# Program order for ScalarE, VectorE and GpSimd in the seven-product groups of a decoder trunk, with bank reads ahead of operand preparation

## The chip, the cores and the metric

The kernel runs on one core of one Trainium2 chip. The metric is device time of one execution in microseconds (us). The engines are TensorE (PE in the profile; PEld are its weight loads), VectorE (DVE), ScalarE (ACT), GpSimd (POOL) and SyncE (SP), which issues most loads. Each engine takes its instructions from a queue of its own, in the order in which the built program has them, and waits on semaphores for the others.

## The reference, cut to what matters

Two layers work on a stream of 512 tokens by 1024 features. The part that the change touches is the gated feed-forward block:

```python
gu = x @ w_gate_up[l]                                  # 1024 -> 2 x 2816
hidden = jax.nn.silu(gu[..., :D_FF]) * gu[..., D_FF:]
x = _layer_norm(DEEPNORM_ALPHA * x + hidden @ w_down[l], ln2_g[l], ln2_b[l])
```

All is float32. To keep that precision on TensorE the kernel splits every operand in a high and a low part and makes three matmuls of each product: high x high, high x low and low x high.

## The kernel before

The program runs each layer as a list of weight units of 128 x 1024 floats. For each unit SyncE loads a raw tile (`wraw`, L177 or L179), ScalarE casts it to its high part (`whi`, L204), and VectorE subtracts to get the low part (`wlo`, L137, the helper `lo_of` that all low parts share). There are five raw tiles and five pairs of high and low parts, and preparation runs four operands ahead of TensorE: `used()` is called after each product and prepares the next operand in line.

Of the 22 feature tiles of 128 in the gate and in the up projection, the first two are computed plainly. The other twenty are done two at a time, in ten groups of a layer, each with **seven products** where eight would be usual. A group takes a 2 x 2 arrangement of weight blocks: the two halves of the 1024 inputs, by gate and up. The raw tiles are f (first half, gate), e (second half, up), m (first half, up) and g (second half, gate). The operands come from them in place (L189 to L195):

| product, in TensorE's order | operand | made by | bank |
|---|---|---|---|
| p1 | B11 = f | load | a |
| p3 | B22 = e | load | e |
| p5 | T1: f += m | VectorE L189 | c |
| p7 | T3: m += e | VectorE L191 | d |
| p6 | T2: f += e | VectorE L193 | b |
| p2 | B21 = g | load | a, added on |
| p4 | T4: f += g | GpSimd L195 | d, added on |

f is one tile through T1, T2 and T4, so each sum must wait until the cast and the low part of the one before it have read f. Each product is 24 matmuls (L305). The function `quad_ev` reads the banks (name of the product, then line): p1 L928 and p5 L930, copies by ScalarE to `qa`; p7 L932, VectorE, which takes bank d from the copy of c; p6 L935, VectorE, then L936 and L938 on GpSimd, with the read of bank e (L937, VectorE) between them; p2 L940, silu by ScalarE; p4 L943, VectorE, L944, silu by ScalarE, and two multiplies on GpSimd into the hidden tiles (L950). For the last three hidden tiles of a layer the multiply is L953, and ScalarE (L955) and VectorE (L137, `hd_late`) split the result at once. p4 adds onto bank d, so it can't start before L932 has read it.

What sets the order: TensorE and SyncE run in the order in which the code is written (`manual_schedule`). ScalarE, VectorE and GpSimd are ordered by a scheduler when the program is built, within what the data allow. GpSimd and VectorE share the work on the raw tiles: L195 writes f, so it waits for the low part of T2.

Of the kernel before, what the change touches and what calls it, by code (L numbers as in the profile page):

```python
# [13 lines left out]
ALU = mybir.AluOpType  # L14
# [11 lines left out]
FT = DFF // P  # L26
# [82 lines left out]
def decoder_trunk(ctx: ExitStack, tc: tile.TileContext, wall, xT_in, x_in, pvec, lnp, rtab, out):  # L109
    nc = tc.nc  # L110
# [11 lines left out]
    def main_bank():  # L122
        return psm.tile([P, 512], F32, tag="m", name="pm")

    def aux_bank():
        return psa.tile([P, 512], F32, tag="a", name="pa")

    def scratch(shape, name):
        return reg.tile(shape, F32, tag="sc", name=name, bufs=4)

    def bigpair(which, name):
        h = big.tile([P, KT, S], F32R, tag=f"{which}h", name=f"{name}h")
        l = big.tile([P, KT, S], F32R, tag=f"{which}l", name=f"{name}l")
        return h, l

    def lo_of(out_lo, full, hi):
        nc.vector.tensor_tensor(out=out_lo, in0=full, in1=hi.bitcast(F32), op=ALU.subtract)  # L137
# [60 lines left out]
    def prep_to(n):  # L198
        while state["prep"] < min(n, total, state["used"] + NRING):
            i = state["prep"]  # L200
            kind, unit = operands[i]
            r = operand_of(kind, unit)
            hi = wp.tile([P, UNIT], F32R, tag="hi", name="whi")
            nc.scalar.copy(hi, r)  # L204
            lo = None
            if kind == "I":
                half = lambda t: t.rearrange("p (k m) -> p k m", k=KT)[:, :, P // 2 :]
                lo_of(half(hi), half(r), half(hi))
            else:
                lo = wp.tile([P, UNIT], F32R, tag="lo", name="wlo")  # L210
                lo_of(lo, r, hi)
            prep_t[i] = (hi, lo)
            for k in ends.get(i, ()):
                del raw_t[k]
            state["prep"] += 1
            issue_dma(state["dma"] + NRAW - len(raw_t))

    def take():
        i = state["next"]
        state["next"] += 1  # L220
        prep_to(i + 1)
        return prep_t.pop(i)

    def used(n=1):
        state["used"] += n
        prep_to(state["used"] + LOOK)
# [4 lines left out]
    def slot():  # L231
        while side:
            try:
                next(side[0])
                return
            except StopIteration:
                side.popleft()
# [47 lines left out]
    def quad(xh, xl, sh, sl, ev):  # L285


        t1, t2 = slice(0, S // 2), slice(S // 2, S)
        banks = {n: main_bank() if n != "b" else aux_bank() for n in "aecdb"}
        x1, x2 = slice(0, 4), slice(4, 8)  # L290
        for name, act, bank, first in (("p1", (x1, t1), "a", True), ("p3", 3, "e", True), ("p5", 0, "c", True),
                                       ("p7", 2, "d", True), ("p6", 1, "b", True), ("p2", (x2, t1), "a", False),
                                       ("p4", (x2, t2), "d", False)):
            w = take()
            hi, lo = (t.rearrange("p (j k m) -> p j k m", j=2, k=4) for t in w)
            if isinstance(act, int):
                ah, al = sh[:, act], sl[:, act]
            else:
                ah, al = xh[:, act[0], act[1]], xl[:, act[0], act[1]]
            for j in range(2):  # L300
                pm = banks[bank][:, j * 256 : (j + 1) * 256]
                for k in range(4):
                    go = first and j == 0 and k == 0
                    for n, (x, y) in enumerate(((hi, ah), (hi, al), (lo, ah))):
                        nc.tensor.matmul(pm, lhsT=x[:, j, k], rhs=y[:, k], start=go and n == 0,  # L305
                                         stop=j == 1 and k == 3 and n == 2, skip_group_check=not first)
                slot()
            used()
            ev(name, banks)

    def first_units(evacs):

# [79 lines left out]
    for n in (1, 1, 2, 2, 2):  # L392
        t = scratch([P, n, S], "xraw")
# [136 lines left out]
    for l in range(L):  # L530
# [258 lines left out]
        for b in range(NB):  # L789
            t = scratch([P, DM], "xr")  # L790
# [75 lines left out]
        x1h, x1l = bigpair(oth, f"x1{l}")  # L866
# [11 lines left out]
        def hidden(j):  # L878
            tag = ("vh", "vl", "gt", "oo", "qk")[j // 4]
            if tag not in hf_t:  # L880
                hf_t[tag] = reg.tile([P, 4, S], F32, tag=tag, name=f"hf_{tag}")
            return hf_t[tag], j % 4
# [16 lines left out]
        sh, sl = (t.rearrange("p (s m) (c t) -> p s (m c) t", s=4, c=2) for t in bigpair(cur, f"s{l}"))  # L899
# [22 lines left out]
        def quad_ev(j):  # L922
            t = {}

            def ev(name, banks):
                two = lambda n: t.setdefault(n, scratch([P, 2, S], n))
                if name == "p1":
                    nc.scalar.copy(two("qa")[:, 0], banks["a"])  # L928
                elif name == "p5":
                    nc.scalar.copy(two("qa")[:, 1], banks["c"])  # L930
                elif name == "p7":
                    nc.vector.tensor_tensor(out=two("qb")[:, 1], in0=t["qa"][:, 1], in1=banks["d"], op=ALU.subtract)  # L932
                elif name == "p6":
                    u, v = t["qa"][:, 0], t["qa"][:, 1]
                    nc.vector.tensor_tensor(out=u, in0=banks["b"], in1=u, op=ALU.add)  # L935
                    nc.gpsimd.tensor_tensor(out=v, in0=v, in1=u, op=ALU.subtract)  # L936
                    nc.vector.tensor_tensor(out=t["qb"][:, 0], in0=banks["e"], in1=v, op=ALU.add)  # L937
                    nc.gpsimd.tensor_tensor(out=t["qb"][:, 1], in0=t["qb"][:, 1], in1=u, op=ALU.subtract)  # L938
                elif name == "p2":
                    nc.scalar.activation(two("qc")[:, 0], banks["a"], AF.Silu)  # L940
                elif name == "p4":
                    g = t["qc"]
                    nc.vector.tensor_tensor(out=g[:, 1], in0=banks["d"], in1=t["qa"][:, 0], op=ALU.add)  # L943
                    nc.scalar.activation(g[:, 1], g[:, 1], AF.Silu)  # L944
                    up, g = (x.rearrange("p h (j t) -> p j h t", j=2) for x in (t["qb"], g))
                    for i in range(2):
                        if j + i < NHF:
                            w, n = hidden(j + i)
                            w = w[:, n].rearrange("p (h t) -> p h t", h=2)
                            nc.gpsimd.tensor_tensor(out=w, in0=up[:, i], in1=g[:, i], op=ALU.mult)  # L950
                        else:
                            n = 2 * (j + i - NHF)
                            nc.gpsimd.tensor_tensor(out=up[:, i], in0=up[:, i], in1=g[:, i], op=ALU.mult)  # L953
                            hh, hl = (late[:, n + q].rearrange("p (h t) -> p h t", h=2) for q in range(2))
                            nc.scalar.copy(hh, up[:, i])  # L955
                            lo_of(hl, up[:, i], hh)
            return ev

        for j in range(2, FT, 2):
            quad(x1h, x1l, sh, sl, quad_ev(j))  # L960

        hid = {j: (late[:, 2 * (j - NHF)], late[:, 2 * (j - NHF) + 1]) for j in range(NHF, FT)}
        place = {"next": 0}
# [25 lines left out]
        for b in range(NB):  # L989
            t = scratch([P, DM], "xr2")  # L990
# [103 lines left out]
```

## Time and profile before

| what | value |
|---|---|
| time, median of 3 runs | 1809.02 us (1807.4 to 1809.77) |
| the profiled execution's own time; its span | 1809.39 us; 1807.7 us |
| granted TensorE clock in the span | 0.997 |
| low parts, L137 `wlo` | 380 instructions, mean 1223 ns, 461.3 us busy |
| casts, L204 | 367 instructions, mean 1049 ns, 382.4 us busy |
| matmuls of the groups | L305, 20 groups, in two stretches of the span, from 573.3 and from 1469.2 us |
| GpSimd sums L195 | 20, mean 2535 ns |
| GpSimd L936 and L938 | 20 each, mean 2142 and 1288 ns |

The profile is of one execution on the one core. Its times are from the span's start. A row of the timeline gives start, duration, engine, line, operation, output and inputs, and in brackets the idle time ahead of it with what ended it; "x2" joins two instructions that follow each other. Line numbers are those of the kernel before; behind L938 the changed kernel's differ by one or so, since lines moved.

### The profile page before, as it was taken

Reading aid. Unit: us, or ns where it says so; the run is one execution under the profiler, and the core shown is the slowest. Engines: PE = TensorE matmul, PEld = TensorE weight load, DVE = VectorE, ACT = ScalarE, POOL = GpSimd, SP = SyncE. Lnnn points to the kernel's source line nnn. Section 1 sums busy time; section 2 is a strip of 40 time slices with the busy share of each in tenths; the row PEclk is TensorE's granted clock in tenths of the full one; section 3 lists DMA queues with packets and bytes.
Section 4 is the critical chain, followed back from the end, with each engine's and each line's share of the span. In section 5 each row is a group of like instructions: output and inputs, shape, how many; then the busy total and the mean of one; then the engine's idle time right before and its main releaser. Section 6 shows DMA issues by size and latency. Waiting matters only on the chain.

```text
span 1807.7 us, 24819 instructions
## 1 busy us (share of the span) xinstructions
PE 1783.2 (99%) x10040; PEld 1561.5 (86%) x10040; DVE 1072.7 (59%) x1582; ACT 738.5 (41%) x1056; POOL 298.5 (17%) x245
## 2 busy tenths in 40 slices
PE   9999999999999999999999999999999999999998
PEld 7888888888889999988898888888888899999886
DVE  6655236654459777773476642467535687767634
ACT  4434326554225444451244343356433254444410
POOL 2020000010001444430020100010100014444200
PEclk9999999999999999999999999999999999999999
DMA  7222243234323322363242222422443223322621
GB/s 246 94 82 73 91 153 103 82 129 152 97 93 108 100 94 94 96 220 97 90 163 90 86 82 93 163 82 80 132 162 93 94 94 102 109 94 94 222 70 47
DMA packets 65268, 200.95 MB, mean 111 GB/s; under 512 B 6233, under 2 KB 8153, under 8 KB 63105
## 3 DMA queue, kind: packets, MB, share of 16 engines
q1 hardware_dynamic: 58768, 168.32, 28.6%
q0 software_dynamic: 6384, 31.04, 4.9%
q8 instruction: 79, 1.29, 0.3%
q14 instruction: 37, 0.29, 0.1%
HBM read 186.73 MB, written 12.60 MB: 110 GB/s over the span
## 4 chain that ended last, share of the span: by engine, by line
PE 85%; DVE 6%; POOL 4%; issue 3%; ACT 1%; DMA 0%; SPq 0%; DVEq 0%; POOLq 0%
PE pm L247 10%; PE pm L248 10%; PE pm L249 10%; PE pm L305 10%; PE pm L332 9%; PE pm L334 9%; PE pm L333 9%; PE pa L333 3%; PE pa L332 3%; PE pa L334 3%; DVE wlo L137 2%; PE pa L305 2%; POOL wraw L195 1%; POOL qa L936 1%; PE pa L465 1%
## 5 line engine op out<-in xcount | busy, mean ns | idle before, releaser
L137 DVE TENSOR_TENSOR wlo<-wraw,whi 128x1024 fp32r<-128x1024 f32 (+2 forms) x380 | 461.3, 1223 | 412.5 <-ACT whi L204 410.5
L204 ACT CAST whi<-wraw 128x1024 fp32r<-128x1024 f32 x367 | 382.4, 1049 | 699.2 <-PE pm L248 224.8
L421 POOL TENSOR_TENSOR rs<-ve,nhalf 128x4 f32<-128x4 f32 (+1 forms) x32 | 32.1, 1003 | 639.0 <-DVE ve L420 639.0
L247 PE MATMUL pm<-x20h,whi 128*128 128x512 f32 (+1 forms) x288 | 107.0, 372 | 0.0
L249 PE MATMUL pm<-x20h,wlo 128*128 128x512 f32 (+1 forms) x288 | 105.5, 366 | 0.0
L248 PE MATMUL pm<-x20l,whi 128*128 128x512 f32 (+1 forms) x288 | 105.4, 366 | 0.0
L332 PE MATMUL pm<-whi,x0h 128*128 128x512 f32 x256 | 102.4, 400 | 1.8 <-DVE rvl L137 1.7
L332 PE MATMUL pm<-whi,x20h 128*128 128x512 f32 x256 | 102.4, 400 | 0.6 <-DVE rvl L137 0.6
L334 PE MATMUL pm<-wlo,x20h 128*128 128x512 f32 x256 | 100.4, 392 | 0.0
L334 PE MATMUL pm<-wlo,x0h 128*128 128x512 f32 x256 | 100.3, 392 | 0.0
L333 PE MATMUL pm<-whi,x0l 128*128 128x512 f32 x256 | 100.1, 391 | 0.0
L333 PE MATMUL pm<-whi,x20l 128*128 128x512 f32 x256 | 100.1, 391 | 0.0
L247 PE MATMUL pm<-x0h,whi 128*128 128x512 f32 x232 | 91.9, 396 | 0.0
L249 PE MATMUL pm<-x0h,wlo 128*128 128x512 f32 x232 | 90.5, 390 | 0.0
L248 PE MATMUL pm<-x0l,whi 128*128 128x512 f32 x232 | 90.4, 390 | 0.0
L305 PE MATMUL pm<-x10h,whi 128*128 128x256 f32 x240 | 68.6, 286 | 5.0 <-DVE qb L932 5.0
L305 PE MATMUL pm<-x11h,whi 128*128 128x256 f32 x240 | 68.6, 286 | 5.0 <-DVE qb L932 5.0
L936 POOL TENSOR_TENSOR qa<-qa 128x512 f32<-128x512 f32 x20 | 42.8, 2142 | 163.1 <-DVE qa L935 129.7
L305 PE MATMUL pm<-s1h,whi 128*128 128x256 f32 x240 | 68.4, 285 | 0.0
L305 PE MATMUL pm<-s0h,whi 128*128 128x256 f32 x240 | 68.4, 285 | 0.0
L305 PE MATMUL pm<-s1l,whi 128*128 128x256 f32 x240 | 68.0, 283 | 0.0
L305 PE MATMUL pm<-s1h,wlo 128*128 128x256 f32 x240 | 68.0, 283 | 0.0
(452 smaller groups left out, 4940.7 us busy)
## 6 DMA issues: line engine op xcount, KB each, us to landing
wraw<-wall SPq DMA_DIRECT2D x307, 512.0 KB, 3.6
yd<-sga POOLq DMA_DIRECT2D x4, 1024.0 KB, 5.0
ya<-yd POOLq DMA_DIRECT2D x4, 1024.0 KB, 6.1
gb<-lnp POOLq DMA_DIRECT2D x4, 1024.0 KB, 5.2
x1d<-xr POOLq DMA_DIRECT2D x8, 512.0 KB, 3.0
xr<-x1d POOLq DMA_DIRECT2D x8, 512.0 KB, 4.7
negm<-md POOLq DMA_DIRECT2D x2, 1026.0 KB, 7.2
xr<-xtok POOLq DMA_DIRECT2D x4, 512.0 KB, 4.1
```

The costliest lines, as they stand in the source:

```text
L137: nc.vector.tensor_tensor(out=out_lo, in0=full, in1=hi.bitcast(F32), op=ALU.subtract)
L195: nc.gpsimd.tensor_tensor(out=f, in0=f, in1=g, op=ALU.add)
L204: nc.scalar.copy(hi, r)
L247: nc.tensor.matmul(pm[:, c0:c1], lhsT=hi[:, k], rhs=xh[:, k, c0:c1], start=(k == 0), stop=False)
L248: nc.tensor.matmul(pm[:, c0:c1], lhsT=hi[:, k], rhs=xl[:, k, c0:c1], start=False, stop=False)
L249: nc.tensor.matmul(pm[:, c0:c1], lhsT=lo[:, k], rhs=xh[:, k, c0:c1], start=False, stop=(k == KT - 1))
L305: nc.tensor.matmul(pm, lhsT=x[:, j, k], rhs=y[:, k], start=go and n == 0, stop=j == 1 and k == 3 and n == 2, skip_group_check=not first)
L332: nc.tensor.matmul(pm, lhsT=sh(k)[:, a], rhs=hi[:, j], start=first, stop=False)
L333: nc.tensor.matmul(pm, lhsT=sl(k)[:, a], rhs=hi[:, j], start=False, stop=False)
L334: nc.tensor.matmul(pm, lhsT=sh(k)[:, a], rhs=lo[:, j], start=False, stop=last)
L421: nc.gpsimd.tensor_tensor(out=rs[:, :n], in0=ve[:, :n], in1=nhalf[:, :n], op=ALU.pow)
L936: nc.gpsimd.tensor_tensor(out=v, in0=v, in1=u, op=ALU.subtract)
```

## The change

```diff
@@ quad
                 slot()
+            ev(name, banks)
             used()
-            ev(name, banks)
@@ quad_ev
                     u, v = t["qa"][:, 0], t["qa"][:, 1]
                     nc.vector.tensor_tensor(out=u, in0=banks["b"], in1=u, op=ALU.add)
                     nc.gpsimd.tensor_tensor(out=v, in0=v, in1=u, op=ALU.subtract)
-                    nc.vector.tensor_tensor(out=t["qb"][:, 0], in0=banks["e"], in1=v, op=ALU.add)
                     nc.gpsimd.tensor_tensor(out=t["qb"][:, 1], in0=t["qb"][:, 1], in1=u, op=ALU.subtract)
                 elif name == "p2":
                     nc.scalar.activation(two("qc")[:, 0], banks["a"], AF.Silu)
+                    nc.vector.tensor_tensor(out=t["qb"][:, 0], in0=banks["e"], in1=t["qa"][:, 1], op=ALU.add)
@@ the loop over the groups
-        for j in range(2, FT, 2):
-            quad(x1h, x1l, sh, sl, quad_ev(j))
+        with tc.manual_schedule(engines={mybir.EngineType.Activation, mybir.EngineType.DVE, mybir.EngineType.Pool}):
+            for j in range(2, FT, 2):
+                quad(x1h, x1l, sh, sl, quad_ev(j))
```

In the code a product's banks are now read before the next operand is prepared, and the read of bank e stands with p2 instead of p6. Inside the loop the three scheduled engines now issue in the order of the code. GpSimd's order comes out as it was: L195, two subtractions, two multiplies.

VectorE, before, from the third group into the fourth (`wraw_4933` is the next group's f, `wraw_5100` its m, `wraw_5059` its e; `wlo` rows name the operand's raw tile):

```order
L189 TENSOR_TENSOR wraw_4933<-wraw_4933,wraw_5100 128x1024
L932 TENSOR_TENSOR qb_5195<-qa_5102,pm_5069 128x512
L137 TENSOR_TENSOR wlo_5223<-wraw_5059,whi_5221 128x1024
L191 TENSOR_TENSOR wraw_5100<-wraw_5100,wraw_5059 128x1024
L935 TENSOR_TENSOR qa_5102<-pa_5070,qa_5102 128x512
L137 TENSOR_TENSOR wlo_5256<-wraw_4933,whi_5254 128x1024
L937 TENSOR_TENSOR qb_5195<-pm_5067,qa_5102 128x512
L193 TENSOR_TENSOR wraw_4933<-wraw_4933,wraw_5059 128x1024
L137 TENSOR_TENSOR wlo_5287<-wraw_5100,whi_5285 128x1024
L943 TENSOR_TENSOR qc_5258<-pm_5069,qa_5102 128x512
L137 TENSOR_TENSOR wlo_5327<-wraw_4933,whi_5325 128x1024
```

Three more low parts (B21, T4 and the next B11) stand behind these rows, and then the ring of rows begins again. VectorE now, at the same place (f is `wraw_4937`, m `wraw_5104`, e `wraw_5066`; the read of bank e has line 940 now):

```order
L137 TENSOR_TENSOR wlo_5165<-wraw_4708,whi_5163 128x1024
L932 TENSOR_TENSOR qb_5193<-qa_5097,pm_5071 128x512
L137 TENSOR_TENSOR wlo_5197<-wraw_4937,whi_5195 128x1024
L935 TENSOR_TENSOR qa_5097<-pa_5072,qa_5097 128x512
L137 TENSOR_TENSOR wlo_5228<-wraw_5066,whi_5226 128x1024
L940 TENSOR_TENSOR qb_5193<-pm_5069,qa_5097 128x512
L189 TENSOR_TENSOR wraw_4937<-wraw_4937,wraw_5104 128x1024
L137 TENSOR_TENSOR wlo_5260<-wraw_4937,whi_5258 128x1024
L943 TENSOR_TENSOR qc_5254<-pm_5071,qa_5097 128x512
L191 TENSOR_TENSOR wraw_5104<-wraw_5104,wraw_5066 128x1024
L137 TENSOR_TENSOR wlo_5293<-wraw_5104,whi_5291 128x1024
L193 TENSOR_TENSOR wraw_4937<-wraw_4937,wraw_5066 128x1024
```

The low parts of T2, B21 and T4 follow. L932 now stands directly behind T4's low part, ahead of B11's low part and of L189. L189 moved from ahead of L932 to behind the read of bank e, L191 from ahead of L935 to behind L943, and L193 from ahead of T3's low part to behind it.

ScalarE, before, one round from the cast of the next group's B11:

```order
L204 CAST whi_5420<-wraw_5163 128x1024
L930 COPY qa_5331<-pm_5297 128x512
L204 CAST whi_5450<-wraw_5289 128x1024
L204 CAST whi_5483<-wraw_5163 128x1024
L204 CAST whi_5514<-wraw_5329 128x1024
L940 ACTIVATE qc_5487<-pm_5295 128x512
L204 CAST whi_5555<-wraw_5163 128x1024
L944 ACTIVATE qc_5487<-qc_5487 128x512
L204 CAST whi_5588<-wraw_5362 128x1024
L928 COPY qa_5561<-pm_5525 128x512
```

ScalarE now (the silu of p2 has line 939 now):

```order
L930 COPY qa_5326<-pm_5299 128x512
L204 CAST whi_5392<-wraw_4937 128x1024
L204 CAST whi_5424<-wraw_5167 128x1024
L204 CAST whi_5455<-wraw_5295 128x1024
L939 ACTIVATE qc_5483<-pm_5297 128x512
L204 CAST whi_5487<-wraw_5167 128x1024
L944 ACTIVATE qc_5483<-qc_5483 128x512
L204 CAST whi_5521<-wraw_5333 128x1024
L928 COPY qa_5556<-pm_5527 128x512
L204 CAST whi_5559<-wraw_5167 128x1024
```

The copy of p5 stands ahead of the casts of T4 and B11 instead of behind them; the cast of T1 moved behind the silu of p2, that of T3 behind L944, and that of T2 behind the copy of p1.

VectorE in the ninth group of a layer, now, where the first late hidden tile is made:

```order
L943 TENSOR_TENSOR qc_6631<-pm_6448,qa_6474 128x512
L137 TENSOR_TENSOR hd_late_4606<-qb_6570,hd_late_4606 128x512
L191 TENSOR_TENSOR wraw_6481<-wraw_6481,wraw_6443 128x1024
L137 TENSOR_TENSOR wlo_6672<-wraw_6481,whi_6670 128x1024
L193 TENSOR_TENSOR wraw_6314<-wraw_6314,wraw_6443 128x1024
```

Before, L191 and L193 stood ahead of this L943, and the low part of the late tile came behind that of T2.

## Prediction

> **What bounds the kernel now.** I read the page's head first, then TensorE's waits, then the stage that they point to.
>
> ```profile
> span 1807.7 us, 24819 instructions
> PE 1783.2 (99%) x10040; PEld 1561.5 (86%) x10040; DVE 1072.7 (59%) x1582; ACT 738.5 (41%) x1056; POOL 298.5 (17%) x245
> ```
> ```profile
> PE pm L305 <- DVE qb L932: 10.0, 12, 0.8
> ```
> ```profile
> 573.30:782.50 209.20, 204.21 (x1683) 202.23 (x1682) 153.16 (x142) 95.13 (x118) 88.80 (x47) 1.00 0.31 104
> 1469.20:1678.40 209.20, 204.21 (x1682) 202.16 (x1681) 153.14 (x142) 95.12 (x118) 88.80 (x47) 1.00 0.32 105
> 651.95:673.40 21.45, 20.59 (x168) 20.26 (x168) 15.10 (x16) 9.14 (x12) 9.46 (x5) 1.00 0.28 98
> ```
>
> TensorE is busy nearly throughout. Its one repeated wait in the groups is p4, which must wait until VectorE has read bank d (L932). The windows (length, then PE, PEld, DVE, ACT, POOL) show the ten groups of both layers: 209.20 us each, 20.9 per group, and 21.45 in a later group. The timeline of TensorE says what a group would need:
>
> ```profile
> 587.60 0.28 PE L305 MATMUL pa<-s0h,wlo 128*128 128x256 f32 x1
> ...
> 672.21 0.28 PE L305 MATMUL pm<-x10l,whi 128*128 128x256 f32 x1
> 672.33 0.28 PE L305 MATMUL pm<-x10h,wlo 128*128 128x256 f32 x1
> 673.45 0.39 PE L305 MATMUL pm<-x10h,whi 128*128 128x256 f32 x1 [0.84 <-DVE qb L932]
> ...
> 782.50 0.39 PE L332 MATMUL pa<-whi,hd_pp 128*128 128x512 f32 x1
> ```
>
> A group is 168 matmuls (the third window's count), and without a wait they start 0.12 us apart (672.21, 672.33): 168 x 0.12 = 20.16 us a group, 2.88 for each of its seven products. So the groups lose 209.2 - 201.6 = 7.6 us a layer, 15.2 in all. That is all there is to gain.
>
> Who sets 21.45? The chain of waits over two groups (start, duration) returns to L932 without once passing through TensorE:
>
> ```profile
> 672.72 0.68 DVE qb L932
> ...
> 676.41 2.15 POOL qa L936
> ...
> 679.19 1.68 DVE wraw L193
> ...
> 682.01 0.61 DVE qc L943
> ...
> 684.87 2.27 POOL hf_gt L950
> 687.14 2.37 POOL wraw L195
> ...
> 689.53 1.06 ACT whi L204
> ...
> 694.15 0.68 DVE qb L932
> ```
>
> 694.15 - 672.72 = 21.43. It is a ring of VectorE, GpSimd and ScalarE; TensorE only follows. **The question is what the ring's length becomes, not how soon one bank is read.** The rows of its members:
>
> ```profile
> 601.41 3.42 DVE L137 TENSOR_TENSOR wlo<-wraw,whi 128x1024 fp32r<-128x1024 f32 x1
> ...
> 657.76 1.68 DVE L193 TENSOR_TENSOR wraw<-wraw 128x1024 f32<-128x1024 f32 x1
> 659.37 1.21 DVE L137 TENSOR_TENSOR wlo<-wraw,whi 128x1024 fp32r<-128x1024 f32 x1
> 660.50 0.68 DVE L943 TENSOR_TENSOR qc<-pm,qa 128x512 f32<-128x512 f32 x1
> ...
> 669.18 2.36 DVE L137 TENSOR_TENSOR wlo<-wraw,whi 128x1024 fp32r<-128x1024 f32 x2 [4.63 <-ACT whi L204]
> 671.57 1.22 DVE L189 TENSOR_TENSOR wraw<-wraw 128x1024 f32<-128x1024 f32 x1
> ...
> 675.59 0.68 DVE L935 TENSOR_TENSOR qa<-pa,qa 128x512 f32<-128x512 f32 x1
> 676.19 1.22 DVE L137 TENSOR_TENSOR wlo<-wraw,whi 128x1024 fp32r<-128x1024 f32 x1
> ```
> ```profile
> 579.53 3.30 POOL L195 TENSOR_TENSOR wraw<-wraw 128x1024 f32<-128x1024 f32 x1 [20.84 <-DVE wlo L137]
> ...
> 600.88 2.87 POOL L195 TENSOR_TENSOR wraw<-wraw 128x1024 f32<-128x1024 f32 x1
> ...
> 661.99 3.71 POOL L950 TENSOR_TENSOR hf_gt<-qb,qc 128x512 f32<-128x512 f32 x2 [3.63 <-ACT qc L944]
> 665.67 2.40 POOL L195 TENSOR_TENSOR wraw<-wraw 128x1024 f32<-128x1024 f32 x1
> 676.41 2.14 POOL L936 TENSOR_TENSOR qa<-qa 128x512 f32<-128x512 f32 x1 [8.35 <-DVE qa L935]
> 678.51 1.29 POOL L938 TENSOR_TENSOR qb<-qb,qa 128x512 f32<-128x512 f32 x1
> ```
> ```profile
> 659.55 1.05 ACT L204 CAST whi<-wraw 128x1024 fp32r<-128x1024 f32 x1 [3.61 <-DVE wraw L193]
> 661.21 0.64 ACT L944 ACTIVATE qc<-qc 128x512 f32<-128x512 f32 x1 [0.61 <-DVE qc L943]
> 668.10 2.00 ACT L204 CAST whi<-wraw 128x1024 fp32r<-128x1024 f32 x2 [4.83 <-POOL wraw L195]
> ```
>
> Three readings. (1) Durations when nothing interferes: VectorE over 1024 columns 1.22, the next instruction 1.14 after its start; a bank read 0.68, the next 0.60 later; cast 1.05; GpSimd 1.29 over 512 columns and 2.40 over 1024. (2) Hand-offs: sum to cast 0.11 (659.44 to 659.55), cast to low part 0.03, L943 to silu 0.03, VectorE or ScalarE to GpSimd 0.14 (676.27 to 676.41), GpSimd to the others 0.03. (3) VectorE instructions with two SBUF inputs and GpSimd's exclude each other: the low part at 601.41 took 3.42 because L195 ran until 603.75, and then needed 1.08; L195 at 579.53 took 3.30 instead of 2.40, and L936 took 2.14 instead of 1.29 at 676.41, each behind a low part that had started first. The one behind starts when the other has held the pair, 1.08 from a low part's start.
>
> On (3) the Trainium skill, "SBUF — State Buffer", section "Who interferes with whom", says that a VectorE instruction with two SBUF inputs and a GpSimd one that reads SBUF contend for a shared pair, and that issue order decides who fully blocks. The three rows agree. Without that rule the new ring would be 20.55, as the first rival works out.
>
> **The change, part by part.** It adds no arithmetic. It removes the freedom of the three queues, which had let the sums L189, L191 and L193 stand ahead of the bank reads. It moves the low part of B11 behind L932. GpSimd's order stays. The new order, with those prices, gives this timetable from a group's L943 (0) to the next; "k+1" operands are the next group's:
>
> | engine, step | start | end | held by |
> |---|---|---|---|
> | DVE L943 | 0 | 0.68 | |
> | ACT silu L944 | 0.71 | 1.35 | |
> | DVE sum T3 (L191) | 0.60 | 1.82 | |
> | POOL first multiply | 1.49 | 2.97 | L191, to 1.68 |
> | ACT cast T3 | 1.93 | 2.98 | |
> | POOL second multiply | 2.97 | 4.26 | |
> | DVE low T3 | 3.01 | 5.34 | that multiply |
> | DVE sum T2 (L193) | 5.26 | 6.48 | VectorE's queue |
> | ACT cast T2 | 6.59 | 7.64 | |
> | DVE low T2 | 7.67 | 8.89 | |
> | DVE low B21 | 8.81 | 10.03 | |
> | POOL L195 | 8.99 | 12.25 | T2's low part, then B21's, to 9.88 |
> | ACT cast T4 | 12.28 | 13.33 | |
> | DVE low T4 | 13.36 | 14.58 | |
> | DVE L932 | 14.50 | 15.18 | VectorE's queue |
> | DVE low B11 | 15.10 | 16.31 | |
> | DVE L935 | 16.23 | 16.91 | VectorE's queue |
> | POOL L936 | 17.05 | 19.19 | low B22, begun 16.83 |
> | DVE bank e | 19.22 | 19.91 | |
> | DVE sum T1 (L189) | 19.83 | 21.56 | GpSimd's second subtraction, to 20.48 |
> | ACT cast T1 | 21.67 | 22.72 | |
> | DVE low T1 | 22.75 | 23.97 | |
> | DVE L943 | **23.89** | | VectorE's queue |
>
> The read of bank d does come earlier relative to B11's low part and L189. But L932 still stands behind T4's low part, and T4 needs L195, which needs T2's low part to have been read:
>
> ```profile
> POOL wraw L195 <- DVE wlo L137: 41.7, 2, 20.8
> ```
>
> In the kernel before, the hoisted L193 was done before L943, and L195 had that wait in the first group of a layer alone. Now sum, cast and low part of T3, T2 and T1 run one after another in one queue, each cast leaving VectorE idle, and none is beside the bank reads. **The ring becomes 23.9, 2.5 longer than 21.43**, and well over TensorE's 20.16. TensorE is not part of it: its p6 starts at 8.94 at the earliest, p2 11.82, p4 waits until 15.23 and is done at 18.4, before L943's turn. New waits show at p7 (low part of T3, 5.34) and p6 (low part of T2, 8.89), besides p4.
>
> Sum for a layer, on the profiled execution's clock. In the first group p6's last matmul ends at 587.60 + 0.28 = 587.88, so L935 is at 588.0 and the next L943 7.66 later (23.89 - 16.23), at 595.7. Eight rings: 595.7 + 8 x 23.9 = 786.9 is the ninth group's L943. Its second half goes to the late tiles, whose cast and low part now stand before L191 in the queues:
>
> ```profile
> L955 ACT CAST hd_late<-qb x6: 620/622/622, 771.9 to 1690.1; 128x512 fp32r<-128x512 f32 x6
> L137 DVE TENSOR_TENSOR hd_late<-qb,hd_late x6: 691/1129/2249, 772.6 to 1690.8; 128x512 fp32r<-128x512 f32 x6
> ```
>
> Two multiplies end at 4.07, the cast at 4.72, the low part lets go at 5.36; T3's low part then frees VectorE at 8.91 instead of 5.26: 3.65 more. L932 of the tenth group: 786.9 + 14.5 + 3.65 = 805.05, p4 starts at 805.8 and ends its 24 matmuls at 808.7. The stage after starts there and not at 782.50: **26.2 us a layer**. The second layer's window is as long as the first's, so 52.4.
>
> At nothing: the weight loads,
>
> ```profile
> DMA to landing us min/median/max: 3.4/3.8/5.6
> ```
>
> since m of the next group is loaded once T2's low part is done (8.89), lands near 13 and is first needed by L189 at 19.83; 6 us of cover would have to go before it costs. ScalarE's new order too: its casts wait for sums anyway. The splits of the hidden tiles after the groups lie beside down-projection matmuls of the stage after, as before. The first group's own T2 to T4 are prepared as before.
>
> The profiled execution took 1809.39 (span 1807.7 and 1.7 around it), 0.4 over the median. 1809.4 + 52.4 = 1861.8.
>
> **Rivals.** *Faster: the exclusion does not bite.* If GpSimd and VectorE ran side by side, the holds in the table would fall away: T3's low part 1.1 earlier, L195 0.9 more, L936 0.9, L189 0.6, together 3.35: a ring of 20.55. Then L943 is at 594.3 in the first group (6.3 after L935) and at 758.7 in the ninth; the late tiles cost 4.8 (L191 at 5.36, not 0.60); L932 comes 12.5 after L943 in that ring, at 776.0; p4 ends at 779.6, so 2.9 us a layer are gained: 1803.6. The sign turns at a ring of about 20.9. Against it: the 3.42 row. For it: nothing but the change's small parts. Beyond it lies the ring under 20.16, with all 15.2 gained, 1794. "PSUM — Partial Sum Buffer" in the Trainium skill, section "Summary: rules for kernel authors", says to evacuate promptly, which speaks for the change; no run here yet shows a bank read alone moved, and the ring says that the read was not what held it.
>
> *No change: the ring keeps 21.43*, if the queues' new order put the sums in VectorE's idle 4.63 us (row 669.18) rather than in its way: 1809. The order printed on VectorE has them after L943, against this.
>
> *Slower by less: GpSimd wins the ties.* If L195 went ahead of B21's low part, 0.85 would go from each ring: 9 x 0.85 x 2 = 15.3, 1846.5. Speaking for it: 0.18 us decide; against it: the 3.30 row, where that pair stood so and L195 lost. *Slower by more*: 20 hand-offs a ring at 0.03 more each: 0.6 x 9 x 2 = 10.8, 1872.6.
>
> **How the numbers follow.** Forecast, 1855 to 1867: 0.66. Slower by less, 1838 to 1855: 0.14. Slower by more, up to 1876: 0.08. Faster by the missing exclusion or more: 0.08. No change: 0.04. The range 1842 to 1874 takes in the tie and the hand-offs and leaves out about 0.15. 0.2% of the time, 3.6 us, is what a measurement of this kernel tells from no change: faster 0.08, same 0.04, slower 0.88.
>
> **What would show it.** L932 to L932 23.9 us apart, in place of 21.43; the groups' window 235 us, in place of 209.20; TensorE idle at p7 and p6 behind low parts (L137), p4 still behind L932; L195 waiting for a low part in all 20 groups and not 2; L193 after T3's low part. Wrong would be: a ring under 21.5, or L189, L191 and L193 running while VectorE would otherwise wait.

## The result, and the profile after

| kernel | median | range | runs |
|---|---|---|---|
| before | 1809.33 us | 1807.4 to 1809.77 | 4 |
| after | 1859.23 us | 1858.53 to 1861.83 | 4 |

The ratio is 1.0281 (95% interval 1.0263 to 1.0298): slower, 0.1% under the predicted 1861.8. The profiled execution took 1861.83. The head of the page after, the windows over the first layer's ten groups and over one later ring (columns as in the prediction), TensorE's waits in the groups, and GpSimd's wait at L195:

```profile
span 1860.1 us, 24795 instructions
PE 1795.1 (97%) x10040; PEld 1566.4 (84%) x10040; DVE 1079.3 (58%) x1582; ACT 739.7 (40%) x1056; POOL 296.9 (16%) x245
```
```profile
574.75:809.37 234.62, 209.46 (x1682) 204.63 (x1681) 154.10 (x141) 93.73 (x117) 89.19 (x47) 0.99 0.27 91
682.90:706.72 23.82, 20.93 (x170) 20.35 (x168) 15.76 (x15) 9.12 (x12) 9.43 (x5) 1.00 0.27 91
```
```profile
PE pm L305 <- DVE wlo L137: 26.4, 16, 1.8
PE pm L305 <- ACT whi L204: 18.1, 16, 4.5
PE pa L305 <- DVE wlo L137: 5.6, 14, 0.4
```
```profile
POOL wraw L195 <- DVE wlo L137: 133.7, 20, 20.8
```

VectorE has nearly the same work (1079.3 us busy, 1072.7 before), and a layer's groups take 25.4 us more: 234.62 instead of 209.20 (the second layer's the same). Of TensorE's waits, the first row is p7 and the third p6 (the bank `pa`), each behind a low part. The second names L204, but 14 of its 16 waits, of 0.65 us each, are p4 waiting for L932. (The two of 4.5 us are p7 of a layer's tenth group, behind T3's cast, which the late tile delays.) The row of one of these p4, which starts right behind the read that ends at 682.90 + 0.68 = 683.58:

```profile
683.73 0.36 PE L305 MATMUL pm<-x10h,whi 128*128 128x256 f32 x1 [0.65 <-ACT whi L204]
```

The chain of waits over one ring, from one L932 to the next (start, duration). T4's cast ended at 680.67 + 1.06 = 681.73, long ahead of that matmul:

```profile
680.67 1.06 ACT whi L204
...
682.90 0.68 DVE qb L932
683.58 1.13 DVE wlo L137
684.71 0.61 DVE qa L935
...
685.46 2.15 POOL qa L936
...
688.24 1.71 DVE wraw L189
690.03 1.06 ACT whi L204
691.11 1.22 DVE wlo L137
692.33 0.60 DVE qc L943
692.94 1.14 DVE wraw L191
...
694.14 1.06 ACT whi L204
695.23 2.31 DVE wlo L137
697.54 1.15 DVE wraw L193
...
698.76 1.06 ACT whi L204
699.84 1.24 DVE wlo L137
...
701.15 3.33 POOL wraw L195
704.50 1.06 ACT whi L204
...
706.72 0.68 DVE qb L932
```

It has sum, cast and low part three times over (L189, L191, L193), end to end, and then L195. Before, the three sums stood between the bank reads, each ahead of the low part that came next. The chain never touches TensorE, as in the kernel before.

### The profile page after: what moved, and what is told of

It is laid out like the page before. It is cut to its first block, busy times and chain, and to the rows that moved or that the text cites. A ratio compares the mean times of both kernels' runs of the same rounds, so it can differ in the third digit from the quotient of the medians.

```text
span 1860.1 us, 24795 instructions
## 1 busy us (share of the span) xinstructions
PE 1795.1 (97%) x10040; PEld 1566.4 (84%) x10040; DVE 1079.3 (58%) x1582; ACT 739.7 (40%) x1056; POOL 296.9 (16%) x245
## 4 chain that ended last, share of the span: by engine, by line
PE 78%; DVE 11%; POOL 5%; ACT 4%; issue 2%; DMA 0%; SPq 0%; DVEq 0%; ACTq 0%; POOLq 0%
PE pm L249 10%; PE pm L247 10%; PE pm L248 10%; PE pm L332 9%; PE pm L334 9%; PE pm L333 9%; DVE wlo L137 5%; PE pm L305 5%; ACT whi L204 3%; PE pa L333 3%; PE pa L332 3%; PE pa L334 3%; POOL wraw L195 3%; POOL qa L936 2%; DVE wraw L189 1%
## 5 line engine op out<-in xcount | busy, mean ns | idle before, releaser
L137 DVE TENSOR_TENSOR wlo<-wraw,whi 128x1024 fp32r<-128x1024 f32 (+2 forms) x380 | 467.5, 1239 | 460.5 <-ACT whi L204 459.0
L204 ACT CAST whi<-wraw 128x1024 fp32r<-128x1024 f32 x367 | 379.1, 1049 | 717.1 <-PE pm L248 224.8
L195 POOL TENSOR_TENSOR wraw<-wraw 128x1024 f32<-128x1024 f32 x20 | 66.3, 3316 | 133.7 <-DVE wlo L137 133.7
L305 PE MATMUL pm<-s0h,wlo 128*128 128x256 f32 x240 | 69.4, 289 | 13.3 <-DVE wlo L137 13.3
L305 PE MATMUL pm<-s1h,wlo 128*128 128x256 f32 x240 | 69.4, 289 | 13.1 <-DVE wlo L137 13.1
L305 PE MATMUL pm<-s1h,whi 128*128 128x256 f32 x240 | 69.2, 288 | 4.5 <-ACT whi L204 4.5
L305 PE MATMUL pm<-s0h,whi 128*128 128x256 f32 x240 | 69.0, 288 | 4.5 <-ACT whi L204 4.5
L305 PE MATMUL pm<-x11h,whi 128*128 128x256 f32 x240 | 68.6, 286 | 4.6 <-ACT whi L204 4.6
L305 PE MATMUL pm<-x10h,whi 128*128 128x256 f32 x240 | 68.6, 286 | 4.6 <-ACT whi L204 4.6
```

The source lines that it names most:

```text
L195: nc.gpsimd.tensor_tensor(out=f, in0=f, in1=g, op=ALU.add)
```

## The experiments

All times are medians; each ratio is to the kernel before, run beside it on the same chip. "Ring" is the distance of two reads of bank d (L932) on VectorE from the third group on.

| kernel | time, us | ratio, 95% interval | ring, us |
|---|---|---|---|
| before | 1809.33 | 1 | 21.43 |
| code order alone | 1811.03 | 1.0004 (0.9994 to 1.0014) | 21.44 |
| program order alone | 1870.78 | 1.0342 (1.0326 to 1.0357) | 24.43 |
| both: after | 1859.23 | 1.0281 (1.0263 to 1.0298) | 23.82 |
| after, T2's sum moved up | 1838.85 | 1.0164 (1.0149 to 1.0179) | 22.40 |
| after, late split moved down | 1853.84 | 1.0247 (1.0232 to 1.0263) | 23.81 |
| after, VectorE left free | 1833.13 | 1.0128 (1.0113 to 1.0143) | 22.24 |
| after, T4's sum on VectorE | 1828.09 | 1.0104 (1.0089 to 1.0119) | 21.78 |
| before, bank d's read moved up | 1809.06 | 0.9997 (0.9987 to 1.0006) | 21.42 |
| sums early | 1798.20 | 0.9942 (0.9925 to 0.9958) | 20.72 |
| sums early, T4's sum first | 1793.29 | 0.9910 (0.9895 to 0.9925) | 20.16 |

### Which half of the change does it

The first half alone is the change without the `with tc.manual_schedule(...)` line. Built, it has the order of before on VectorE, ScalarE and GpSimd in the groups, because the scheduler orders them anew.

> Only the first half of the change: in the code the bank reads stand ahead of the operand preparation (and bank e's read in p2's step), with all engines left to the scheduler as before. The built program then has the order of before on VectorE, ScalarE and GpSimd in the groups. Theory, that program order makes the loss: 1809 (1806.5 to 1811.5), ring 21.4. Rival, that the code's order alone changes something else (buffers, semaphores): over 1815.

Measured: 1811.03, no difference. The second half alone keeps `used()` ahead of `ev(...)` and the read of bank e in p6's step, as before:

```diff
-        for j in range(2, FT, 2):
-            quad(x1h, x1l, sh, sl, quad_ev(j))
+        with tc.manual_schedule(engines={mybir.EngineType.Activation, mybir.EngineType.DVE, mybir.EngineType.Pool}):
+            for j in range(2, FT, 2):
+                quad(x1h, x1l, sh, sl, quad_ev(j))
```

> Only the second half of the change: the three engines issue in program order, but the code keeps the order of before, each operand's preparation ahead of the bank read, and bank e in p4's step. On VectorE the sums stand right ahead of their own low parts here too (L189, low part T1, L191, low part T3, then the last bank read, L193, low part T2, B21, T4). Theory, that program order (sum, cast, low part of T1, T3, T2 one after another in VectorE's queue) lengthens the ring and the bank reads' place does not: ring about 24.5, 1862 to 1869 with the late tiles' share. Rival, that the bank reads ahead of the preparations cause the loss: as before, 1809, ring 21.4.

Measured: 1870.78, slower than the whole change, and 2 us over what was expected (the ring of 24.43 was expected at 24.5). Bank e is read in p6's step here, and not in p4's as the expectation has it. VectorE's rows in one ring, the low parts of T1 and T3 with T3's sum between them:

```profile
689.48 1.23 DVE L137 TENSOR_TENSOR wlo<-wraw,whi 128x1024 fp32r<-128x1024 f32 x1 [1.19 <-ACT whi L204]
690.62 1.22 DVE L191 TENSOR_TENSOR wraw<-wraw 128x1024 f32<-128x1024 f32 x1
693.00 1.23 DVE L137 TENSOR_TENSOR wlo<-wraw,whi 128x1024 fp32r<-128x1024 f32 x1 [1.16 <-ACT whi L204]
```

The pattern is the same: each sum is followed by its own low part, and VectorE idles 1.2 us for the cast between them. So **program order, with the code's order as it is, makes the loss, and the first half of the change (the bank reads ahead of the preparation, bank e's in p2's step) takes 11.5 us of it back** (1870.78 - 1859.23). The rival that blames the bank reads falls.

### Is it VectorE's order, and which links

One instruction is moved: T2's sum (L193) directly behind T3's (L191).

```diff
         elif kind == "T3":
             nc.vector.tensor_tensor(out=m, in0=m, in1=e, op=ALU.add)
-        elif kind == "T2":
             nc.vector.tensor_tensor(out=f, in0=f, in1=e, op=ALU.add)
```

> One instruction moved on VectorE in the kernel after: the sum of T2 (L193) stands directly behind the sum of T3 (L191), ahead of T3's low part. Ring theory: L193 is done about 4.0 after L943 and not 6.48, so T2's low part ends at about 7.6 and not 8.9 and L195 starts 1.3 earlier, though T3's low part now comes 1.1 LATER (6.4 and not 5.3) since it queues behind L193. Ring 22.4 instead of 23.8; 1835 us (1830 to 1842). Rival, that what is lost is the sum of TensorE's own waits (at p7 behind T3's low part 2.1, at p6 0.7, at p4 0.9 a group, which add up to the 3.7 by which 23.8 exceeds 20.16): T3's low part 1.1 later makes the longest of these waits longer, 1.1 x 9 x 2 = 20 us slower than after, 1879. If neither counts: 1859.

Measured: 1838.85, ring 22.40; 20.4 us faster than after, and not 20 slower. VectorE's rows (L192 is L193 here, each line behind it one less), and TensorE's wait:

```profile
685.71 1.22 DVE L191 TENSOR_TENSOR wraw<-wraw 128x1024 f32<-128x1024 f32 x1
686.85 2.32 DVE L192 TENSOR_TENSOR wraw<-wraw 128x1024 f32<-128x1024 f32 x1
689.09 4.56 DVE L137 TENSOR_TENSOR wlo<-wraw,whi 128x1024 fp32r<-128x1024 f32 x3
```
```profile
PE pm L304 <- DVE wlo L137: 22.0, 16, 2.0
```

The longest of TensorE's waits did become longer (2.0 instead of 1.8), and the kernel faster. Where TensorE waits is not where the time is made here: its waits only absorb what the ring leaves. Three low parts now run in one piece, without the idle 1.2 us between T3's and T2's.

With VectorE alone given back to the scheduler (the set of engines has no `DVE`), the sums are hoisted again:

> The kernel after with ScalarE and GpSimd in program order and VectorE left to the scheduler; ScalarE's and GpSimd's orders are those of after. On VectorE the sums are hoisted again (L189 behind B22's low part, L191 behind L935, L193 behind T1's low part). Theory, that VectorE's order alone makes the ring long: ring 22.2, 1822 to 1830. Rival, that ScalarE's program order (a cast waiting at the head of the queue, the copies behind it) makes it: 1855 to 1861.

Measured: 1833.13, ring 22.24 as expected for VectorE's order. The time is 3 us above the expected span. The groups hold all of the loss: they take 220.0 and 221.0 us in the two layers instead of 209.2, together 22.6 more, and the profiled span is longer by as much (1830.3 instead of 1807.7). The ring into the tenth group, with the late tile, has 4.7 of this in each layer: it took 24.40, and 19.71 in the kernel before. More than half of the loss (26.1 of 49.9) hangs on VectorE's order alone, with ScalarE's and GpSimd's as in after. How the rest divides between ScalarE's order and the order that VectorE got here (it is not that of before) was not separated. That ScalarE's has a part in it is suggested by the trace, and not shown: T3's sum ends at 678.66 + 1.22 = 679.88, but its cast starts at 685.81, behind the silu L944 in ScalarE's queue, and VectorE then idles 1.63 us for that cast.

T4's sum on the other engine:

```diff
-            nc.gpsimd.tensor_tensor(out=f, in0=f, in1=g, op=ALU.add)
+            nc.vector.tensor_tensor(out=f, in0=f, in1=g, op=ALU.add)
```

> The kernel after with T4's sum (L195) on VectorE instead of GpSimd, at the same place in the program. It adds 1.1 us of work to VectorE a group, and takes from GpSimd the 3.3 us that L195 takes there with its hold. Ring theory, with VectorE and GpSimd excluding each other: the hand-over T2's low part to T4's cast shortens from 4.7 (7.67 to 12.28) to 3.6, ring 22.8, 1841 (1836 to 1846). Rival, without exclusion: 20.3, about 1800. Rival, that more work on VectorE, the engine that all wait for, makes its ring longer: 24.9, 1879.

Measured: 1828.09, ring 21.78: faster than expected by 13 us. The chain shows why:

```profile
690.63 1.24 DVE wlo L137
...
691.89 1.24 DVE wraw L195
...
693.21 1.06 ACT whi L204
```

From T2's low part to T4's cast it takes 2.58 (690.63 to 693.21), not 3.6: on VectorE, L195 stands ahead of B21's low part, and I had put it behind. That mistake is the 1.0 by which the ring is shorter than expected. That the engine which all wait for got more work and the kernel faster is the plainest sign that the ring, and not VectorE's load, sets the time. Without exclusion the ring was expected at 20.3; it is not seen here.

The late tile's split is moved in the code to the head of the next group's p7 step. That is right ahead of the read of bank d, and not behind it as the expectation says:

```diff
-                            nc.scalar.copy(hh, up[:, i])
-                            lo_of(hl, up[:, i], hh)
+                            splits.append((hh, hl, up[:, i]))
...
+                if name == "p7":
+                    late_splits()
```

> The kernel after, but the cast and the low part that split a late tile of the ninth group stand behind the tenth group's read of bank d instead of ahead of T3's preparation. Late-tile theory: the ring between the ninth and the tenth group is 23.8 like the others instead of 27.4, so 3.6 a layer less: 7.2 us, 1852 (1850.5 to 1853.5). Rival, that the first groups' slack or another operation (the two multiplies that end the group, T3's cast) makes that ring long: 1859.

Measured: 1853.84; the ring into the tenth group fell from 27.43 to 24.42 (reads at 776.42 and 800.84), 3.0 of the 3.6. VectorE's rows there (L942 is L932):

```profile
800.24 0.69 DVE L137 TENSOR_TENSOR hd_late<-qb,hd_late 128x512 fp32r<-128x512 f32 x1
800.84 0.68 DVE L942 TENSOR_TENSOR qb<-qa,pm 128x512 f32<-128x512 f32 x1
```

The missing 0.6 is the split's low part itself (800.24 to 800.84), which stands right ahead of the read, on the chain.

### The bank read by itself

The order of before is written out, with one thing moved on VectorE, the read of bank d. Two things go with it: ScalarE's copy of p5, which that read needs, stands ahead of T4's cast, and the late tiles' split comes later, in p7's step. VectorE's order:

```diff
 low part of T4
+L932  read of bank d
 low part of B11
 L189  sum of T1
-L932  read of bank d
 low part of B22
 L191  sum of T3
 L935
```

> The kernel before with its instruction order of the groups written out (the three engines in program order), and one thing changed: the read of bank d (L932 of before) stands ahead of B11's low part and of the sum L189 on VectorE, 2.3 us earlier. It is the change's intent alone. Ring theory: L932 is no link that matters, since the same instructions still run on VectorE between T4's low part and L935; the ring stays 21.4, p4 waits no longer for L932 but TensorE waits elsewhere in the group; 1809 (1806 to 1812). Rival, that bank d's read gates TensorE (its one repeated wait in the kernel before): the wait goes, the group falls to 20.2, 1794 (1793 to 1798). Rival, that program order as such costs: as after, 1840 to 1860.

Measured: 1809.06, ratio 0.9997. The window over a layer's groups, and TensorE's waits in them (L329 is L305, L229 is L204, L972 is p2's silu):

```profile
572.72:781.61 208.89, 204.47 (x1682) 202.22 (x1681) 149.72 (x141) 93.19 (x115) 88.86 (x46) 1.00 0.31 102
```
```profile
PE pm L329 <- ACT whi L229: 5.8, 12, 0.5
PE pm L329 <- ACT qc L972: 3.0, 10, 0.3
```

The rows of T4's low part, of the read of bank d (L961 is L932) and of p4's first matmul:

```profile
669.60 1.23 DVE L138 TENSOR_TENSOR wlo<-wraw,whi 128x1024 fp32r<-128x1024 f32 x1 [4.62 <-ACT whi L229]
670.74 0.68 DVE L961 TENSOR_TENSOR qb<-qa,pm 128x512 f32<-128x512 f32 x1
```
```profile
671.57 0.36 PE L329 MATMUL pm<-x10h,whi 128*128 128x256 f32 x1 [0.48 <-ACT whi L229]
```

The first wait names L229, but it is p4 again, as in the kernel after: T4's cast ended at 669.57, and the read at 670.74 + 0.68 = 671.42, just ahead of the matmul. So the expectation that p4 would no longer wait for bank d was wrong: that wait became shorter, 5.8 us in all instead of 10.0, and a second one, behind p2's silu, came beside it. Against the ring p4 does start 2.3 us earlier: 1.97 after the start of T4's low part (671.57 - 669.60) instead of 4.27 (673.45 - 669.18 in the kernel before). Still the ring is 21.42 and the groups take 208.89. The read's place doesn't set the time. Nor does program order cost as such, since all three engines are in it here. The Trainium skill, "PSUM — Partial Sum Buffer", section "Summary: rules for kernel authors", says to evacuate promptly, and gives as its reason that "2 MiB is tight", which is about room; for the time of this kernel an evacuation some 2.3 us earlier gave nothing.

### A ring shorter than TensorE's work

An order written by hand, under the same program order as the change. `SU`, `CA` and `LO` are sum, cast and low part of an operand, by its number from the group's first (5 is B21, 6 T4; 7 to 13 are the next group's B11, B22, T1, T3, T2, B21, T4); `R` is a bank read or what is done with it, and a late tile's split waits for the next p7:

```python
"p1": [R("a1"), CA(5), LO(5)],
"p3": [],
"p5": [R("c"), CA(6), LO(6), CA(7), LO(7)] + [SU(9)] * more,
"p7": [R("d1"), CA(8), LO(8)] + [SU(10)] * more + [late_split],
"p6": [R("b"), R("g2"), CA(9), LO(9)] + [SU(11)] * more,
"p2": [R("a2"), R("e"), CA(10)],
"p4": [R("d2")] + [CA(11)] * more + [R("silu")] + [LO(11)] * more + [LO(10)] + [SU(13)] * more + [R("mult")],
```

> All three engines in program order as in the change, but an order written by hand: each sum one to two operands ahead of its cast (L189's sum behind B11's low part, L191's behind B22's, L193's behind T1's, all ahead of the bank reads that follow), the last bank read right behind bank e's, GpSimd's sum of T4 ahead of the two multiplies, the late tiles' split later. Ring theory: the ring is then below TensorE's 20.16, so TensorE runs without waits: groups 201.6 us a layer, 15 under the kernel before, 1794 (1792 to 1798). Rival, that program order itself costs (each engine waits for its oldest instruction whatever the order): 1830 to 1860. Rival, that GpSimd and VectorE exclude each other for longer where the sums stand beside L195: a ring of 20.7 or more, 1800 to 1809.

Measured: 1798.20, ring 20.72, under the kernel before by 0.58% (0.42 to 0.75). The ring is the third theory's figure and not the first's, and the time lies between their ranges (to 1798, and from 1800). But the order built is not the one that was meant, as GpSimd's rows show (L983 are the two multiplies, L196 is L195):

```profile
678.95 3.81 POOL L983 TENSOR_TENSOR hf_gt<-qb,qc 128x512 f32<-128x512 f32 x2 [0.85 <-ACT qc L976]
682.72 3.38 POOL L196 TENSOR_TENSOR wraw<-wraw 128x1024 f32<-128x1024 f32 x1
```

T4's sum is issued with the operand B21 (number 12), not with T4 (13), so `SU(13)` moved nothing. With `SU(12)` in its place:

> The order of the fourth run (opt1_sums_early), in which GpSimd's sum of T4 in fact stayed behind the two multiplies (it was issued with B21 and not with T4, so the ring there is that of its second rival, 20.7), with that sum now really ahead of the two multiplies, behind T2's low part. Ring theory: T4's cast starts 2.6 earlier, the ring falls below TensorE's 20.16, the groups take 201.6 to 202 us, 1 to 1.5 a layer less: 1795 (1793 to 1797.5). Rival, that the two multiplies then stand in the way of B21's low part and of T4's low part on VectorE, and the ring stays 20.7: 1798.

Measured: 1793.29. GpSimd's rows, and the window over a layer's groups:

```profile
675.08 3.32 POOL L196 TENSOR_TENSOR wraw<-wraw 128x1024 f32<-128x1024 f32 x1 [1.33 <-DVE wlo L138]
678.35 3.54 POOL L983 TENSOR_TENSOR hf_gt<-qb,qc 128x512 f32<-128x512 f32 x2
```
```profile
571.07:772.67 201.60, 201.60 (x1683) 201.60 (x1681) 171.90 (x145) 97.69 (x120) 107.14 (x49) 1.00 0.34 113
```

Ten groups take exactly 10 x 20.16, and TensorE is busy in all of it. The version is 0.90% faster than the kernel before (0.75 to 1.05) and 3.5% faster than after, though VectorE and GpSimd are busy longer (171.90 and 107.14 a layer instead of 153.16 and 88.80 in the kernel before), holds included.

## Why the prediction was right

**The ring** was predicted at 23.89 and is 23.82. VectorE's rows of after for the first group's L943 and for two steps of a later ring:

```profile
596.97 0.68 DVE L943 TENSOR_TENSOR qc<-pm,qa 128x512 f32<-128x512 f32 x1
```
```profile
692.25 0.68 DVE L943 TENSOR_TENSOR qc<-pm,qa 128x512 f32<-128x512 f32 x1
...
697.46 1.21 DVE L193 TENSOR_TENSOR wraw<-wraw 128x1024 f32<-128x1024 f32 x1
```

Counted from 692.25, with the chain's rows: T3's low part ends at 5.29 (5.34 predicted); L193 starts at 5.21 (5.26); L195 at 8.90 (8.99), and lasts 3.33 (3.26); L932 comes at 14.47 (14.50); L189, counted from the L943 before, at 19.81 (19.83). These links stand where the order put them, each within 0.1.

**The late tile** was put at 3.65 and costs 3.61 (27.43 - 23.82). The moved split confirms that it is this, not something else in that group.

**The sum** was 26.2 a layer and is 25.4: eight rings shorter by 0.07 make 0.56, and the first L943 comes 22.22 after the groups' first matmul (596.97 - 574.75) where the prediction had 22.4. The groups give 50.8; the profiled execution's span is 52.4 longer, since its groups also began 1.4 later (574.75, 573.32 before), with the same work ahead of them. The medians differ by 49.9. So 52.4 was some 2 us too much. That the profiled execution took 1861.83, the forecast's 1861.8 to the digit, is luck: its later start made up for what the sum had too much.

**The signs.** The window (235 predicted, 234.62), waits at p7 and p6 behind low parts, p4 behind L932, L195's wait in 20 groups and L193 behind T3's low part all came.

**The exclusion.** T3's low part lasts 2.31 in the ring, and 1.23 in the tenth group, where the late tile's steps held it up until GpSimd's multiplies were over:

```profile
795.20 1.23 DVE L137 TENSOR_TENSOR wlo<-wraw,whi 128x1024 fp32r<-128x1024 f32 x1 [1.15 <-ACT whi L204]
```

Same instruction, same operands' size, 1.08 apart by whether GpSimd is at work. This is what the Trainium skill states ("SBUF — State Buffer", "Who interferes with whom"), and the trace agrees. The rival without it (1803.6) falls. (Its four terms add to 3.5 as they are printed; the timetable's own ends give 1.11, 0.86, 0.85 and 0.51, so 3.33 and a ring of 20.56, against its 20.55.) *GpSimd wins the ties* falls too: L195 lost to B21's low part in each ring, 3.32 us on the mean of 20 instead of 2.40. *Longer hand-offs* didn't come: sum to cast takes 0.09 (697.46 + 1.21 to 698.76; 0.11 predicted), cast to low part 0.03 (694.14 + 1.06 to 695.23). *No change* belongs to the code order alone.

## What to carry to other kernels

When TensorE follows a ring of other engines, time the ring from the order of the built program and the durations in the trace. Where TensorE waits did not tell here what to move: an earlier read of the bank that it waited for gave nothing, and a move that made its longest wait longer gave 20 us. In an engine that issues in order, an instruction that starts a chain through another engine (here a sum that a cast waits for) belongs one or two operands ahead of the one that ends it, so that the hand-off passes beside other work. In this kernel fixing the order by hand paid only with that distance written in: the same mechanism gave 1859 without it and 1793 with it.

## What the hardware showed beside this

TensorE's granted clock fell after waits of 2 us, and not each time. The rows are matmuls of p7 that came late, one of after and two of the kernel with T2's sum moved up; the windows are those of the matmuls that followed the last two (the clock stands third from the end):

```profile
697.59 0.38 PE L305 MATMUL pm<-s0h,wlo 128*128 128x256 f32 x1 [1.84 <-DVE wlo L137]
```
```profile
669.04 0.39 PE L304 MATMUL pm<-s0h,wlo 128*128 128x256 f32 x1 [1.98 <-DVE wlo L137]
...
691.43 0.39 PE L304 MATMUL pm<-s0h,wlo 128*128 128x256 f32 x1 [1.97 <-DVE wlo L137]
```
```profile
669.04:672.00 2.96, 2.96 (x24) 2.96 (x25) 2.22 (x2) 0.30 (x1) 1.80 (x1) 1.00 0.76 246
691.43:695.00 3.57, 3.57 (x21) 3.57 (x22) 2.22 (x2) 0.30 (x1) 2.41 (x1) 0.68 0.70 220
```

After 1.84 it stayed at 1.00 (the ring's window in the section on the result). After 1.97 and 1.98 it fell in some rings and not in others: behind the row at 669.04 it stayed, and behind the row at 691.43 ten matmuls still start 0.12 apart, and then 16 at 0.21, about 1.5 us more. It cost nothing: the rings stayed at 22.4, and TensorE's next wait was shorter.

The Trainium skill, "TensorE: Matmul & The Clock Gate", Part 1, lowers the clock after an idle window of about 3.4 us; the rows here show falls after less. What decides between the two cases was not tried.
